# Eight modulation vectors of a two-block attention stage, taken from VectorE's multiply-adds to TensorE's float32 products

## The chip, the cores and the metric

The kernel runs on one core of a Trainium2 chip. The metric is device time in microseconds, the median of three runs. The engines named below are TensorE (PE, with its weight loads as PEld), VectorE (DVE), ScalarE (ACT), GpSimd (POOL) and SyncE (SP), which only issues transfers here.

## What is computed

512 tokens of 1,024 channels go through four layers of the same shape. The mixer of the first is MLA and sliding-window attention, of the second differential and forgetting attention, of the last two a convolution and a gated recurrence, each of these with an MLP behind it. Each layer is modulated by vectors that come from a conditioning vector c:

```
ada   = silu(c) @ w_ada + b_ada          # 1024 -> 3 * 1024 for an attention layer
h     = rmsnorm(x, g_pre) * (1 + scale) + shift
x'    = x + gate * rmsnorm(mixer(h) @ w_out, g_post)
```

A vector is 1,024 columns of such a product: 4 MB of float32 weights, read once. This study is about eight of those vectors: gate 0 with its g_post, and scale and shift of the second layer, and one vector for a later layer, all made while the first attention mixer runs; and the gate of the second layer and scale, shift and gate of the third, made while the second attention mixer runs.

## The kernel before

Everything large is a product on TensorE. Each float32 operand is split into a high and a low part and the product is taken as three products of the parts (L207, `mm3`); the splits are made by ACT (L199, L221) and by DVE or POOL (L200, L224). The program is written in layer order, and a list scheduler with a model of its own for times sets the order on each engine. Every engine then takes its instructions strictly in that order: an instruction that waits holds up all that stand behind it on its engine.

The four functions that matter:

- `even` and `odd` are the two attention mixers. Scores go through TensorE (psum tag `sc`), a softmax that alternates between DVE (L596 maximum and mask, L599 reciprocal), ACT (L598 exponential) and POOL (L603 scaling), a transpose of the probabilities on TensorE (L626, tag `tp`) and a product with V (L636, L645, tag `pv`). In between stand products of the weights for gates and projections (tag `mm`), which need no softmax. Query and key heads are transposed by `heads_T` (L613) into the psum tag `tq`, of which there is one bank.
- `ada` queues a vector in eight steps, two halves of 512 columns by four steps of 256 rows. A step loads 256 x 512 weights (512 KB) with one transfer on SP's queue (L497) into one of two buffers called `araw`, and DVE adds two 128 x 512 multiples of it to `acc` (L502 for the first one of a half, L504 for the others). Behind the fourth step of a half four products of a column of ones (L511, each into its own 32 columns of the array) sum `acc` over the partitions, DVE adds the bias (L513) and multiplies by g where there is one (L517), and four transfers of 512 bytes write the row to DRAM (L520).
- `tick` takes the next step from the queue; `group` calls it after each group of products of a weight, the mixers call it after a head, `flush` takes what is left. So the steps lie between the softmaxes in the order of DVE.
- `first` runs a mixer with its four vectors queued before it or by it, and afterwards spreads the rows over the partitions (L547) for the out projection.

In both mixers 32 steps are taken, so the study is about 64 steps, 128 multiply-adds on DVE and 16 groups of four products of ones. The vectors of the later layers use the same function and are not touched.

Of the kernel before, what the change touches and what calls it, by code (L numbers as in the profile page):

```python
# [16 lines left out]
P = 128  # L17
# [9 lines left out]
# layout of the constant array  # L27
# [39 lines left out]
G0 = 2  # L67
LEVELS = (1, 2, 4, 8, 16, 32, 64, 128, 256)
# [8 lines left out]
def constants():  # L77
# [16 lines left out]
    # of a row's block of 32: the columns of each level; of a row's block of 128: the block of 32 on the diagonal  # L94
# [13 lines left out]
def cap4(v, o):  # L108
    """512 elements of a DRAM vector as four rows of 128, each on 32 partitions"""
    return bass.AP(tensor=v.tensor, offset=v.offset + o, ap=[[P, 4], [0, 32], [1, P]])  # L110


class K:
    def __init__(self, tc, h, es):
# [12 lines left out]
        self.ada_pool = ()  # L127
        self.ada_tag, self.ada_raw = "mm", ("araw", 2)
# [18 lines left out]
    def scope(self, **bufs):  # L147
        """a pool of working tiles; bufs by tag"""
# [26 lines left out]
    def oT_tiles(self, t0):  # L175
        """a mixer's output as a split pair: the first token block in t0, the others in the places of the activations
        that the mixer read"""
        act = self.act

        class O:  # L180
            def __init__(self, a):
                self.a = a

            def __getitem__(self, ix):
                _, k, t = ix
                if t.start >= P:
                    return act[self.a][:, k, t]
                return t0[self.a][:, k, t]
        return O(0), O(1)
# [19 lines left out]
    def wgran(self, w, k0, nk, c0, cw, own=False):  # L209
        """weights rows [k0*128, (k0+nk)*128), cols [c0, c0+cw) -> split pair [128, 2, nk, cw]"""  # L210
# [16 lines left out]
    def wload(self, w, c0, cw, kc, own=0):  # L227
        """the weights of kc chunks of channels, the last granules in own tiles of the scope"""
# [9 lines left out]
    def rank(self, off):  # L238
        """instructions that the scheduler takes off places later than their place in the program"""
# [5 lines left out]
    def mark(self):  # L245
        """what comes from the queue of the modulation stays behind the work of DVE so far"""
# [6 lines left out]
    def advance(self, g, have, want):  # L253
        """steps of g until their cost reaches want; the cost so far"""
# [7 lines left out]
    def weave(self, main, n, fill, cost):  # L262
        """n steps of main, with fill of that cost (or of cost(i) after i steps) spread over them, and kept behind
        them on TensorE"""
# [22 lines left out]
    def gemm_xs(self, act, w, c0, cw, kc, evac, tag="mm", subs=None):  # L287
        """out[tok, c0:c0+cw] by token block; evac(tb, psums)"""
# [17 lines left out]
    def gemm_xk(self, act, gs, cw, kc, evac):  # L306
        """as gemm_x, with the channels outermost"""
# [9 lines left out]
    def gemm_tb(self, act, w, evac, after=None, late=None):  # L317
        """out[tok, 0:1024], a token block's two halves one after the other; evac(tb, half, psum). with late,
        the last channels come late: the first half of two token blocks does the others first, the second block after
        that instruction"""  # L320
# [29 lines left out]
    def gemm_ws(self, act, w, c0, cw, kc, evac, tag="mm"):  # L350
        """out[c0:c0+cw, tok] by chunks of 128 channels; evac(chunk, psum)"""
# [14 lines left out]
    def gemm_wh(self, act, jobs):  # L366
        """as gemm_w for jobs (w, c0, evac) of 256 channels, the first half of the tokens before the second"""
# [14 lines left out]
    def rstd(self, ss, n, cols=1):  # L382
        """(ss/n + eps)^-1/2"""
# [8 lines left out]
    def cond(self, cs):  # L392
        """silu of each vector of cs, as columns [128, 8]"""
# [10 lines left out]
    def start(self, x_in, c, c2, w, b, g, wg, cw):  # L404
        """norm and modulation of the first layer: the normalised x channel-major while the modulation's weights
        come in; returns silu(c) and the step that makes chunk k of the split pair"""
# [77 lines left out]
    def ada(self, ccol, w, b, c0, kind, g=None):  # L484
        """one vector of the modulation as a row in DRAM, queued in eight steps"""
# [3 lines left out]

        def step(half, gk):  # L490
            o0 = c0 + half * 512
# [3 lines left out]
            tag, n = self.ada_raw  # L495
            raw = self.wp.tile([P, 2, 512], F32, tag=tag, name=self.nm(tag), bufs=n)
            nc.sync.dma_start(out=raw, in_=w[gk * 256:(gk + 1) * 256, o0:o0 + 512].rearrange("(k p) c -> p k c", p=P))  # L497
# [9 lines left out]
            arow = self.rp.tile([P, P], F32, tag="arow", name=self.nm("arow"), bufs=2)  # L507
            nc.sync.dma_start(out=arow, in_=cap4(b, o0))
# [5 lines left out]
            if g is not None:  # L514
                gr = self.rp.tile([P, P], F32, tag="gr", name=self.nm("gr"), bufs=2)
                nc.sync.dma_start(out=gr, in_=cap4(g, half * 512))
                nc.vector.scalar_tensor_tensor(out=arow, in0=arow, scalar=1.0 if kind == "scale" else 0.0, in1=gr,  # L517
                                               op0=ALU.add, op1=ALU.mult)
            for j in range(4):
                nc.sync.dma_start(out=row[half * 512 + j * P:half * 512 + (j + 1) * P].unsqueeze(0), in_=arow[32 * j:32 * j + 1])  # L520

        def later(h_, q_):
            if STRICT:
                self.mark()
            with self.tc.issue_after(self.gate):
                step(h_, q_)
# [9 lines left out]
    def group(self):  # L536
        """after each group of products of a weight"""
# [3 lines left out]

    def flush(self):
        self.tick(len(self.pend))

# [1243 lines left out]
```

## Time and profile before

| | before |
|---|---|
| time of three runs | 2110.22, 2113.64 (median), 2122.06 us |
| span of the profiled execution | 2106.4 us (its own time is not listed beside it) |
| mean granted TensorE clock | 0.959 |
| busy share of the span | PE 92%, DVE 67%, ACT 42%, POOL 38% |
| transfers | 270.67 MB, 128 GB/s in the mean |
| attention mixers with the 64 steps | about 46 to 700 us |

The median stands 7.2 us above the span of the profiled execution; a span is therefore compared with a span, and 7.2 us is added to get to a time of a run. Busy times are of an execution that was profiled; the granted clock is the share of full speed that TensorE was given, 1.00 for 2.4 GHz and 0.50 for 1.2 GHz.

### The profile page before, as it was taken

How to read it: one execution, taken by the hardware profiler on the slowest of the kernel's cores; microseconds unless marked ns; L12 is line 12 of the kernel's file. 1: busy time of each engine (PE TensorE's matmuls, PEld its weight loads, DVE VectorE, ACT ScalarE, POOL GpSimd, SP SyncE). 2: the span in 40 equal slices, each digit the busy share in tenths (PEclk: the TensorE clock that was granted, in tenths of full speed). 3: DMA queues.
4: the chain of work that ended last, by engine and by line, in shares of the span. 5: the costliest groups of instructions: out<-in, count | busy, mean ns of one | idle time of the engine just before them, and what ended most of it. 6: DMA issues, size and time to landing. Idle time of an engine off the chain costs nothing.

```text
span 2106.4 us, 32096 instructions
## 1 busy us (share of the span) xinstructions
PE 1943.9 (92%) x12471; PEld 1580.0 (75%) x12471; DVE 1402.8 (67%) x1987; ACT 884.5 (42%) x1499; POOL 805.1 (38%) x701
## 2 busy tenths in 40 slices
PE   7799999897999988679899999999999998999998
PEld 5688667664776776448788989876777778898896
DVE  5356775545555769976987648667787858485673
ACT  4245553134544434333525436243454534352452
POOL 1223334222233448615232422455585544223232
PEclk9899979998999999889999999999999999999999
DMA  8384555366343751432554235453322322242331
GB/s 317 121 230 142 173 165 157 88 156 144 87 129 94 250 165 56 110 105 91 170 187 132 83 99 178 132 151 106 101 78 87 116 86 80 90 131 71 121 101 60
DMA packets 225024, 270.67 MB, mean 128 GB/s; under 512 B 26602, under 2 KB 145609, under 8 KB 224872
## 3 DMA queue, kind: packets, MB, share of 16 engines
q1 hardware_dynamic: 188982, 232.83, 36.3%
q10 hardware_dynamic: 35890, 35.79, 5.5%
q8 instruction: 98, 1.61, 0.3%
q14 instruction: 54, 0.44, 0.1%
HBM read 252.46 MB, written 16.12 MB: 128 GB/s over the span
## 4 chain that ended last, share of the span: by engine, by line
PE 49%; DVE 14%; issue 6%; DMA 6%; POOL 4%; ACT 2%; ACTq 0%; POOLq 0%; DVEq 0%; SPq 0%
PE mm L207 28%; PE sc L207 5%; PE mm L1186 4%; PE sc L1186 3%; PE tp L1186 3%; DVE acc L504 3%; DMA araw<-in_ada_w_dram 2%; DVE hl L224 2%; DVE ol L1312 2%; DVE hl L200 1%; DMA raw<-in_od_w_in_dram 1%; DVE X L1547 1%; PE pv L207 1%; DMA raw<-in_ada_w_dram 1%; PE tp L626 1%
## 5 line engine op out<-in xcount | busy, mean ns | idle before, releaser
L207 PE MATMUL mm<-hTh,hl 128*128 128x512 f32 (+1 forms) x1296 | 410.9, 393 | 19.0 <-ACT t L1339 7.0
L207 PE MATMUL mm<-hl,hid 128*128 128x512 f32 x1344 | 317.0, 395 | 5.3 <-DVE hid L200 3.8
L221 ACT CAST hl<-raw 128x1024 fp32r<-128x1024 f32 (+2 forms) x219 | 224.1, 1033 | 223.8 <-PE mm L207 133.8
L207 PEld LDWEIGHTS mm<-hl,hid 128*128 128x128 f32 x1344 | 251.9, 188 | 65.2 <-DVE hid L200 4.9
L207 PEld LDWEIGHTS mm<-hTh,hl 128*128 128x128 f32 x1296 | 242.8, 194 | 74.6 <-ACT t L1339 7.9
L224 DVE TENSOR_TENSOR hl<-raw,hl 128x1024 fp32r<-128x1024 f32 (+2 forms) x186 | 251.3, 1361 | 67.3 <-ACT hl L221 66.8
L207 PE MATMUL mm<-hTl,hl 128*128 128x512 f32 (+2 forms) x648 | 253.2, 391 | 0.9 <-DVE hTl L200 0.8
L207 PE MATMUL mm<-hl,hTh 128*128 128x512 f32 (+3 forms) x752 | 220.5, 371 | 26.9 <-DVE t L584 11.9
L1103 POOL TENSOR_TENSOR xr<-xr,t 128x512 f32<-128x512 f32 x56 | 80.4, 1435 | 303.4 <-DVE t L1100 303.4
L504 DVE SCALAR_TENSOR_TENSOR acc<-araw,ccol,acc 128x512 f32<-128x512 f32 x182 | 158.5, 871 | 45.0 <-DMA araw<-in_ada_w_dram 31.4
L207 PEld LDWEIGHTS mm<-hl,hTh 128*128 128x128 f32 x752 | 140.0, 197 | 52.2 <-ACT t L751 9.6
L603 POOL TENSOR_TENSOR s<-s,sm 128x256 f32<-128x256 f32 (+3 forms) x112 | 82.7, 739 | 184.0 <-DVE sm L599 165.4
L207 PEld LDWEIGHTS mm<-hTl,hl 128*128 128x128 f32 (+1 forms) x648 | 125.6, 194 | 26.4 <-DVE hTl L200 1.5
L199 ACT CAST hl<-raw 128x1024 fp32r<-128x1024 f32 x84 | 86.8, 1048 | 136.1 <-PE mm L207 111.3
L200 DVE TENSOR_TENSOR hl<-raw,hl 128x1024 fp32r<-128x1024 f32 x84 | 131.3, 1578 | 13.5 <-ACT hl L199 12.9
L207 PE MATMUL mm<-hl,hTl 128*128 128x512 f32 (+3 forms) x376 | 138.8, 369 | 0.3 <-DVE hTl L457 0.3
L224 POOL TENSOR_TENSOR hl<-raw,hl 128x1024 fp32r<-128x1024 f32 x33 | 84.3, 2554 | 131.5 <-ACT hl L221 131.4
L1166 POOL TENSOR_TENSOR raw<-raw,raw 128x1024 f32<-128x1024 f32 x28 | 76.2, 2722 | 147.1 <-DVE rows L1166 85.2
L1100 DVE TENSOR_TENSOR t<-mm,rows 128x512 f32<-128x512 f32 x56 | 38.5, 687 | 104.3 <-PE mm L207 104.0
L598 ACT ACTIVATE s<-s,sm 128x256 f32<-128x256 f32 (+5 forms) x128 | 69.6, 544 | 90.7 <-DVE sm L596 86.7
L1312 DVE SCALAR_TENSOR_TENSOR ol<-u,dw,ol 128x512 f32<-128x512 f32 x90 | 103.2, 1147 | 2.9
L207 PE MATMUL sc<-b,b 64*128 64x256 f32 (+7 forms) x384 | 92.2, 356 | 12.5 <-DVE sm L596 11.7
(358 smaller groups left out, 3956.4 us busy)
## 6 DMA issues: line engine op xcount, KB each, us to landing
raw<-in_mlp_w_dram SPq DMA_DIRECT2D x128, 512.0 KB
araw<-in_ada_w_dram SPq DMA_DIRECT2D x72, 512.0 KB
raw<-in_hgrn_w_in_dram SPq DMA_DIRECT2D x40, 512.0 KB
araw<-in_w_ada_dram SPq DMA_DIRECT2D x32, 512.0 KB
raw<-in_od_w_in_dram SPq DMA_DIRECT2D x32, 512.0 KB
raw<-in_ada_w_dram SPq DMA_DIRECT2D x24, 512.0 KB
rows<-row SPq DMA_DIRECT2D x16, 512.0 KB
raw<-in_conv_w_in_dram SPq DMA_DIRECT2D x16, 512.0 KB
```

The costliest lines, as they stand in the source:

```text
L199: nc.scalar.copy(out=hi, in_=src)
L200: nc.vector.tensor_tensor(out=lo, in0=src, in1=hi.bitcast(F32), op=ALU.subtract)
L207: self.nc.tensor.matmul(out, lhsT=lt[a], rhs=rt[b], start=start and n == 0, stop=stop and n == 2)
L221: self.nc.scalar.copy(out=hi, in_=raw[:, :n])
L224: eng.tensor_tensor(out=lo, in0=raw[:, :n], in1=hi.bitcast(F32), op=ALU.subtract)
L504: eng.scalar_tensor_tensor(out=acc, in0=raw[:, k], scalar=c, in1=acc, op0=ALU.mult, op1=ALU.add)
L598: nc.scalar.activation(out=s[:, :m], in_=s[:, :m], func=AF.Exp, scale=-1.0, bias=mn, accum_out=sm)
L603: nc.gpsimd.tensor_tensor(out=p, in0=p, in1=r.to_broadcast([P, n]), op=ALU.mult)
L1103: eng.tensor_tensor(out=xs, in0=xs, in1=t, op=ALU.add)
L1166: eng.tensor_tensor(out=out, in0=x, in1=y, op=f)
L1186: nc.tensor.matmul(ps[:, m * 256:m * 256 + 256], lhsT=ws[n][:, a, k, m * P:m * P + P], rhs=parts[n][b][:, k], start=m + k + t == 0, stop=m ...
L1312: nc.vector.scalar_tensor_tensor(out=yc, in0=u[:, j:j + T], scalar=dw[:, cc, j:j + 1], in1=yc, op0=ALU.mult, op1=ALU.add)
```

## The change

In the two attention mixers, and only there, a step is made on TensorE. After the 512 KB load eight float32 products per step go through the array, for two blocks of 128 rows and four groups of 32 columns: the column of silu(c) stands as the weights, repeated over 32 columns, and a raw 128 x 128 block of `araw` streams through. The eight products of a step gather in the single `tq` bank, and DVE adds the 128 x 128 result to `arow`, which starts as the bias. The products of a step are written one tick later than its load (`ADA_LAG`), and the last ones in `flush`. The bias is now loaded at the first step of a half. The ones, `acc` and its 128 x 512 multiply-adds are gone from these 64 steps.

```diff
+        def step_pe(half, gk):
+            if gk == 0:
+                st[half] = bias(half)
+            raw = load(half, gk)
+            def products():
+                ps = self.psum(self.ada_ps)
+                for k in range(2):
+                    for j in range(4):
+                        nc.tensor.matmul(ps[32 * j:32 * j + 32, :P], lhsT=cap(ccol, gk * 2 + k, [(0, 32)]),
+                                         rhs=raw[:, k, j * P:(j + 1) * P], start=k == 0, stop=k == 1, tile_position=(0, 32 * j))
+                nc.vector.tensor_tensor(out=st[half], in0=ps[:, :P], in1=st[half], op=ALU.add)
+                if gk == 3:
+                    finish(half, st[half])
+            self.ada_late.append(products)
+            self.ada_do(ADA_LAG)
...
-                step(h_, q_)
+                (step_pe if self.ada_pe else step)(h_, q_)
...
+    def ada_do(self, keep):
+        while len(self.ada_late) > keep:
+            self.ada_late.pop(0)()
...
     def flush(self):
         self.tick(len(self.pend))
+        with self.tc.issue_after(self.gate):
+            self.ada_do(0)
...
+                    k.ada_pe = True
...
+                    k.ada_pe = False
```

`load`, `bias` and `finish` hold the lines that `step` had for its load, its bias and the end of a half. The lines of the changed kernel are numbered otherwise: the products of a step stand in L523 and the add in L525, the three-term products in L209, the softmax in L634 (maximum) and L637 (reciprocal), its combination in the differential attention in L1034 and L1035, the transpose of probabilities in L664.

On DVE, in the differential attention of the second mixer, this is the order of before; `s` and `sm` belong to the softmax, `b` is a split pair from the `tq` bank, `acc` and `araw` are the step's:

```order
L596 ISA sm_4299 128x1
L599 RECIPROCAL sm_4301<-sm_4300 128x1
L596 ISA s_4306,sm_4307<-sc_4294,cst 128x128
L596 ISA sm_4307 128x1
L203 SCALAR_TENSOR_TENSOR b_1019_4383<-tq_4378,b_1019_4383 128x512
L599 RECIPROCAL sm_4309<-sm_4308 128x1
L504 SCALAR_TENSOR_TENSOR acc_4550<-araw_4801,ccol_93,acc_4550 128x512
L996 TENSOR_TENSOR sm_4313<-sm_4309,nlam 128x1
L596 ISA s_4350,sm_4351<-sc_4342,cst 128x256
```

At the same place on DVE the order of the change is this:

```order
L634 ISA sm_4531 128x1
L637 RECIPROCAL sm_4533<-sm_4532 128x1
L634 ISA s_4538,sm_4539<-sc_4526,cst 128x128
L634 ISA sm_4539 128x1
L205 SCALAR_TENSOR_TENSOR b_1038_4615<-tq_4610,b_1038_4615 128x512
L637 RECIPROCAL sm_4541<-sm_4540 128x1
L1034 TENSOR_TENSOR sm_4545<-sm_4541,nlam 128x1
L634 ISA s_4582,sm_4583<-sc_4574,cst 128x256
```

The multiply-add that stood ahead of the next softmax is gone; the next add of a step (L525) stands some fifteen rows further on.

On TensorE the order of the change in the first mixer, where the MLA heads end and the sliding window's begin, has products of four steps close together (`araw_2019`, `araw_2123`, `araw_2200` and `araw_2214` are four loads that follow one another through the two buffers):

```order
L209 MATMUL sc_2309<-b_426_1994,b_424_1986 128x256 x3
L523 MATMUL tq_2125<-araw_2019,ccol_93 32x128 x8
L209 MATMUL sc_2247<-b_450_2092,b_448_2084 128x128 x2
L523 MATMUL tq_2202<-araw_2123,ccol_93 32x128 x8
L209 MATMUL sc_2321<-b_450_2092,b_448_2084 128x256 x3
L209 MATMUL sc_2356<-b_426_1994,b_424_1986 128x384 x3
L664 MATMUL tp_2263<-cst,s_2251 128x128
L523 MATMUL tq_2216<-araw_2200,ccol_93 32x128 x8
L209 MATMUL sc_2368<-b_450_2092,b_448_2084 128x384 x3
L664 MATMUL tp_2333<-cst,s_2313 128x128 x2
L683 MATMUL pv_2234<-pt_2265,V_939 64x128
L209 MATMUL sc_2427<-b_426_1994,b_424_1986 128x512 x3
```

Before, there was no instruction on TensorE here that reads `araw`; now a group of eight stands between the scores.

In the sliding-window heads of the first mixer TensorE had one group of ones in such a stretch before (`SV` is the window's V, `acc` the sum of four steps):

```order
L207 MATMUL sc_2919<-b_545_2424,b_634_2702 128x256 x3
L626 MATMUL tp_2842<-cst,s_2828 128x128 x2
L511 MATMUL mm_3252<-acc_3067,ones 32x128 x4
L207 MATMUL sc_2932<-b_545_2424,b_651_2759 128x256 x3
L207 MATMUL sc_2962<-b_545_2424,b_634_2702 128x256 x3
```

It has a step's products after every second or third group of scores in the change:

```order
L664 MATMUL tp_3037<-cst,s_3015 128x128
L523 MATMUL tq_3193<-araw_2997,ccol_93 32x128 x8
L209 MATMUL sc_3102<-b_553_2523,b_643_2813 128x256 x3
L683 MATMUL pv_2768<-pt_2956,SV_753 64x128
L683 MATMUL pv_2768<-pt_2951,SV_753 64x128
L683 MATMUL pv_2768<-pt_2956,SV_753 64x128
L664 MATMUL tp_3041<-cst,s_3028 128x128
L523 MATMUL tq_3207<-araw_3191,ccol_93 32x128 x8
L209 MATMUL sc_3115<-b_553_2523,b_660_2870 128x256 x3
```

So the first mixer's products no longer start with its first gates: the first one stands behind some 490 of TensorE's rows, all 32 steps of this mixer lie in rows 492 to 906, and eleven of them, with the first step of the second mixer as a twelfth, in rows 820 to 915. The 32 of the second mixer lie in rows 915 to 2040, most with 7 to 20 us of other TensorE work between a step and the next but one.

## Rows read from the trace of the kernel before

**Rows 1.** The page's busy times: share of the span, number of instructions.

```profile
PE 1943.9 (92%) x12471; PEld 1580.0 (75%) x12471; DVE 1402.8 (67%) x1987; ACT 884.5 (42%) x1499; POOL 805.1 (38%) x701
```

**Rows 2.** The page's chain that ended last, by engine and by line.

```profile
PE 49%; DVE 14%; issue 6%; DMA 6%; POOL 4%; ACT 2%; ACTq 0%; POOLq 0%; DVEq 0%; SPq 0%
PE mm L207 28%; PE sc L207 5%; PE mm L1186 4%; PE sc L1186 3%; PE tp L1186 3%; DVE acc L504 3%; DMA araw<-in_ada_w_dram 2%; DVE hl L224 2%; DVE ol L1312 2%; DVE hl L200 1%; DMA raw<-in_od_w_in_dram 1%; DVE X L1547 1%; PE pv L207 1%; DMA raw<-in_ada_w_dram 1%; PE tp L626 1%
```

**Rows 3.** Windows of 53 us: busy time of each engine, granted clock, DMA share.

```profile
core 0: us, PE busy (x) PEld busy (x) DVE busy (x) ACT busy (x) POOL busy (x), PEclk, DMA share, GB/s
...
212.00:265.00 53.00, 51.38 (x337) 36.99 (x336) 40.59 (x111) 28.94 (x80) 19.61 (x38) 1.00 0.58 171
265.00:318.00 53.00, 51.16 (x249) 34.27 (x248) 38.04 (x98) 26.90 (x76) 17.41 (x38) 0.74 0.54 169
...
477.00:530.00 53.00, 38.63 (x160) 27.88 (x161) 28.32 (x80) 21.59 (x48) 11.29 (x10) 0.81 0.57 134
```

**Rows 4.** Groups by line on DVE, 30 to 720 us.

```profile
L504 DVE SCALAR_TENSOR_TENSOR acc<-araw,ccol,acc 128x512 f32<-128x512 f32 x127 | 104.4, 822 | 38.1 <-DMA araw<-in_ada_w_dram 25.0 <-DMA araw<-in_w_ada_dram 12.3
...
L513 DVE TENSOR_TENSOR arow<-mm,arow 128x128 f32<-128x128 f32 x16 | 4.6, 288 | 6.3 <-PE mm L511 6.3
```

**Rows 5.** TensorE's timeline: four-column-group products of the kernel's start (two records each).

```profile
start us, us, engine line op out<-in xcount [idle before <-releaser]
...
25.94 0.65 PE L433 MATMUL pv<-wide,rep 128*32 128x128 f32 x16
26.52 0.66 PE L473 MATMUL tp<-cst,t 128*128 128x128 f32 x4
...
30.68 1.08 PE L433 MATMUL tq<-wide,rep 128*32 128x128 f32 x16
31.70 0.69 PE L207 MATMUL mm<-hl,hTl 128*128 128x384 f32 x1
...
35.94 1.08 PE L433 MATMUL tq<-wide,rep 128*32 128x128 f32 x32
36.95 0.44 PE L207 MATMUL mm<-hl,hTh 128*128 128x384 f32 x1
```

**Rows 6.** TensorE's timeline around one group of ones.

```profile
258.39 0.39 PE L207 MATMUL mm<-hTl,hl 128*128 128x512 f32 x1
258.62 0.39 PE L207 MATMUL mm<-hTh,hl 128*128 128x512 f32 x1
258.94 0.42 PE L511 MATMUL mm<-acc,ones 128*32 128x128 f32 x8
259.30 0.43 PE L645 MATMUL pv<-pt,SV 128*64 128x128 f32 x2
```

**Rows 7.** Timeline of SP, DVE and TensorE at 473 to 483 us.

```profile
473.62 0.44 SPq L497 DMA_DIRECT2D araw<-in_ada_w_dram  x1
...
481.56 0.75 DVE L504 SCALAR_TENSOR_TENSOR acc<-araw,ccol,acc 128x512 f32<-128x512 f32 x1 [5.86 <-DMA araw<-in_ada_w_dram]
...
482.78 1.32 PE L207 MATMUL sc<-b,b 64*128 64x384 f32 x3 [6.43 <-DVE sm L596]
```

**Rows 8.** The same engines at 499 to 509 us.

```profile
499.13 0.40 SPq L497 DMA_DIRECT2D araw<-in_ada_w_dram  x1
...
507.47 0.75 DVE L504 SCALAR_TENSOR_TENSOR acc<-araw,ccol,acc 128x512 f32<-128x512 f32 x1 [4.24 <-DMA araw<-in_ada_w_dram]
...
508.55 1.00 PE L207 MATMUL sc<-b,b 64*128 64x256 f32 x3 [3.94 <-DVE sm L596]
```

**Rows 9.** TensorE's timeline: two other waits in the second mixer.

```profile
460.06 0.50 PE L207 MATMUL mm<-hTh,hl 128*128 128x512 f32 x1 [4.24 <-DVE o L668]
...
525.48 0.90 PE L626 MATMUL tp<-cst,s 128*128 128x128 f32 x3 [3.90 <-DMA raw<-in_od_w_in_dram]
```

**Rows 10.** SP's and DVE's timeline in the first mixer's sliding window: two loads.

```profile
278.56 0.40 SPq L497 DMA_DIRECT2D araw<-in_ada_w_dram  x1
...
282.56 0.75 DVE L504 SCALAR_TENSOR_TENSOR acc<-araw,ccol,acc 128x512 f32<-128x512 f32 x1 [0.39 <-DMA araw<-in_ada_w_dram]
...
281.73 0.37 SPq L497 DMA_DIRECT2D araw<-in_ada_w_dram  x1
...
286.35 0.75 DVE L504 SCALAR_TENSOR_TENSOR acc<-araw,ccol,acc 128x512 f32<-128x512 f32 x1 [1.22 <-DMA araw<-in_ada_w_dram]
```

**Rows 11.** Windows of 10 us, columns as in rows 3.

```profile
150.00:160.00 10.00, 7.60 (x38) 6.12 (x37) 8.96 (x19) 4.21 (x12) 4.05 (x3) 0.84 0.70 208
...
280.00:290.00 10.00, 10.00 (x42) 6.31 (x40) 7.34 (x24) 5.15 (x17) 4.19 (x11) 0.50 0.68 216
```

More of the change, by code (lines that the diff above doesn't have):

```diff
@@ L67 @@
 G0 = 2
+ADA_LAG = 1
 LEVELS = (1, 2, 4, 8, 16, 32, 64, 128, 256)
@@ L127, in __init__ @@
         self.ada_pool = ()
+        self.ada_pe, self.ada_late, self.ada_ps = False, [], "tq"
         self.ada_tag, self.ada_raw = "mm", ("araw", 2)
@@ L488, in ada, with load, bias, finish @@
         st = {}
+        def load(half, gk):
+            o0 = c0 + half * 512
+            tag, n = self.ada_raw
+            raw = self.wp.tile([P, 2, 512], F32, tag=tag, name=self.nm(tag), bufs=n)
+            nc.sync.dma_start(out=raw, in_=w[gk * 256:(gk + 1) * 256, o0:o0 + 512].rearrange("(k p) c -> p k c", p=P))
+            return raw
+        def bias(half):
+            arow = self.rp.tile([P, P], F32, tag="arow", name=self.nm("arow"), bufs=2)
+            nc.sync.dma_start(out=arow, in_=cap4(b, c0 + half * 512))
+            return arow
+        def finish(half, arow):
+            if g is not None:
+                gr = self.rp.tile([P, P], F32, tag="gr", name=self.nm("gr"), bufs=2)
+                nc.sync.dma_start(out=gr, in_=cap4(g, half * 512))
+                nc.vector.scalar_tensor_tensor(out=arow, in0=arow, scalar=1.0 if kind == "scale" else 0.0, in1=gr,
+                                               op0=ALU.add, op1=ALU.mult)
+            for j in range(4):
+                nc.sync.dma_start(out=row[half * 512 + j * P:half * 512 + (j + 1) * P].unsqueeze(0), in_=arow[32 * j:32 * j + 1])
+        def step_pe(half, gk):
[5 more added lines that the diff above has]
+                for k in range(2):
+                    for j in range(4):
+                        nc.tensor.matmul(ps[32 * j:32 * j + 32, :P], lhsT=cap(ccol, gk * 2 + k, [(0, 32)]),
[5 more added lines that the diff above has]
+            self.ada_do(ADA_LAG)
         def step(half, gk):
-            o0 = c0 + half * 512
             if gk == 0:
@@ L494, in step @@
             acc = st[half]
-            tag, n = self.ada_raw
-            raw = self.wp.tile([P, 2, 512], F32, tag=tag, name=self.nm(tag), bufs=n)
-            nc.sync.dma_start(out=raw, in_=w[gk * 256:(gk + 1) * 256, o0:o0 + 512].rearrange("(k p) c -> p k c", p=P))
+            raw = load(half, gk)
             for k in range(2):
@@ L506, in step @@
                 return
-            arow = self.rp.tile([P, P], F32, tag="arow", name=self.nm("arow"), bufs=2)
-            nc.sync.dma_start(out=arow, in_=cap4(b, o0))
+            arow = bias(half)
             ps = self.psum(self.ada_tag)
@@ L513, in step @@
             nc.vector.tensor_tensor(out=arow, in0=ps[:, :P], in1=arow, op=ALU.add)
[L514 to L520, printed above, removed]
+            finish(half, arow)
         def later(h_, q_):
```

## The prediction

> **What bounds the kernel now.** I read the busy times first. TensorE is busy for 92% of the span, VectorE for 67% [rows 1], so a microsecond taken from VectorE is worth something only where TensorE waits for it, and a microsecond given to TensorE costs nearly all of itself. The chain that ended last says the same: half of it is TensorE, and the multiply-adds and their loads, the two entries that the change touches, are 3% and 2%, some 100 us together [rows 2]. That is not a gain in waiting: where a chain runs over a multiply-add, TensorE was often busy beside it.
>
> So I went to windows over the two mixers, and there the shares differ. In the first mixer TensorE has hardly a gap: 51.38 of 53 us between 212 and 265 us, though VectorE is at its busiest with 40.59 [rows 3]. From 265 to 318 us it is as full, 51.16, but at a granted clock of 0.74 [rows 3]; inside, from 280 to 290 us, it is busy for all 10 us at 0.50 [rows 11], that is 1.2 GHz, after a wait of the scores on VectorE. In the second mixer there are real gaps: 38.63 of 53 us from 477 to 530, at a clock of 0.81 [rows 3]. VectorE is not full there, 28.32 us; it stands still. The waits tell why: at 481.56 a multiply-add has waited 5.86 us for its load, issued at 473.62, and behind it stands the softmax; TensorE's scores start at 482.78 after 6.43 us of idleness, for that softmax [rows 7]. At 507.47 the same: 4.24 us for a load issued at 499.13, and TensorE 3.94 us later than it could [rows 8]. The order shows the multiply-add ahead of the softmax there before, and gone in the change.
>
> **What it costs on TensorE.** 64 steps of eight products. The trace has the same form (128 rows, 32 columns, 128x128 streamed, two records per product) at the kernel's start: one group of 16 records starts at 25.94 and the next instruction at 26.52, so a step is 0.58 us; a run of two such groups goes from 35.94 to 36.95, 0.505 each; at a lower clock a group takes 30.68 to 31.70, 1.02 [rows 5]. I take 0.58, since nearly every step stands alone: 64 x 0.58 = 37.1 us (32.3 by the packed price). The Trainium skill says in "TensorEngine Tiling (Array Packing)", Tiling Modes, that changing the tiling mode drains TensorE. The trace agrees in size: the lone group is 0.075 us dearer than the packed one; by that rule the sum is the 37.1 taken here, without it 32.3.
>
> Taken away: 16 groups of ones, 258.94 to 259.30, 0.36 each [rows 6], 5.8 us. Left are **+31.3 us**, if all of it lies on TensorE's path. In the second mixer some of it falls into gaps that stay: of the 14.4 us idle from 477 to 530 [rows 3] about 10 are the two waits above; I put **-4** for products that fill the rest and gaps like it.
>
> **What it costs in waits.** *The tq bank.* One bank, shared with the transposes of heads; the next user waits for VectorE's add, 0.29 us (the add behind the ones has the same shape [rows 4]) plus what VectorE has in hand. Most uses are far apart; some six come close (the order shows transposes into tq just ahead of a step): **+2**, 0 to 8.
>
> *Loads that TensorE now waits for itself.* A step's load can start only when the products of the step but one before have read its buffer. Two loads in the sliding window took 282.56 - 278.56 = 4.0 and 286.35 - 281.73 = 4.6 us from issue to use [rows 10]. Between the products on `araw_2019` and those on `araw_2200` the order has 128 x 2 + 256 x 3 + 384 x 3 columns, a step and a transpose. A product of 512 columns takes 0.23 us (258.39 to 258.62 [rows 6]), so that is 1.0 + 0.58 + about 0.2 = 1.8 us, and TensorE would stand still for 2.2 to 2.8. Done so for each step, with the durations of such rows, the steps up to row 761 of the first mixer wait 4.7 us at 4.0 per load and 7.0 at 4.6; part of it lies in gaps that are there anyway: **+4**, 0 to 7. Rows 820 to 915 have some 23 us of work for twelve steps; at full clock they would wait 9 to 13 us.
>
> *That stretch and its clock.* Today its work runs partly at 0.50; from 265 to 318 the lost clock is worth (1 - 0.74) x 51.16 = 13.3 us [rows 3]. If the clock stays up, 13.3 comes back and 9 to 13 goes into waits: -4 to 0. If it stays low, loads are in time, but twelve products cost 1.02 instead of 0.58: +5. I take **0**.
>
> **What it gives back.** VectorE is rid of 127 multiply-adds of 0.82 us, 104.4 us [rows 4], and gets 48 more small adds of 0.29. Where TensorE was the one to wait:
> - 150 to 160 us, eight multiply-adds in a burst: 2.4 us idle, and (1 - 0.84) x 7.60 = 1.2 of clock [rows 11]: **-3.6**.
> - 212 to 265 us: 1.6 us idle [rows 3]: **-1.6**.
> - Second mixer: the two direct waits, 6.43 + 3.94 = 10.4 [rows 7, 8]; of the lost clock from 477 to 530, (1 - 0.81) x 38.63 = 7.3 [rows 3], 80%: 5.8; of the waits of 4.24 and 3.90 [rows 9], which hang on VectorE through other steps or on a weight's transfer, half: 4.1. Together **-20.3**, between -12 and -26.
>
> **Sum.** 31.3 - 4 + 2 + 4 + 0 - 3.6 - 1.6 - 20.3 = +7.8 us. Span 2106.4 + 7.8 = 2114.2; the median stands 7.2 above the span, so 2121.4, say 2121 us: 0.4% slower, within the 0.5% (10.6 us) below which a measurement of this kernel can't tell a change from none.
>
> **Rivals.**
> - *All stalls of VectorE come back, nothing new waits.* Products at the packed price (26.5 net), no tq wait, -4 for gaps, -4 in the sliding window, -3.6 - 1.6, and all of 10.4 + 7.3 + 8.1 = 25.8 in the second mixer: -12.5, thus 2101 us; with the full 13.3 of clock in the sliding window 2092. For it: VectorE's line is on the chain [rows 2]. Against: the price on TensorE is sure, and a clock that rises there makes loads late.
> - *The first mixer starves on its loads* (the other side). Loads of 4.6 us and more, one after the other through two buffers: +7 and +13 in the two dense stretches with the clock low around them so that nothing of the 13.3 returns, tq at +8, and the second mixer gives 16: 31.3 - 4 + 8 + 20 - 3.6 - 16 = +36, 2149 us; halfway between it and the forecast 2135. It decides from a landing of about 4.6 us on. For it: the order's dense places. Against: half clock stretches the work between loads.
> - *The wait only moves.* The loads of 473.62 and 499.13 took 7.9 and 8.3 us [rows 7, 8]; if those of the change are issued no earlier, TensorE waits at L523 instead of VectorE, and the second mixer gives 5 instead of 20.3: +23, 2137 us. Against: 7 to 20 us of work stand between a step and the next but one there, and a softmax no longer stands behind the load.
>
> **How the numbers follow.** The forecast, a balance within 0.5%: 0.36. All stalls back, 2088 to 2103: 0.30. Starved first mixer: 0.20, and the wait that moves: 0.14, both from 2124 to 2149. So faster 0.30, same 0.36, slower 0.34. The range leaves out a tenth at each end: 2088 to 2144; the forecast's own is 2104 to 2124.
>
> **What would show it.** Products at L523 of 0.55 to 0.6 us each at full clock, about 37 us of busy time. In the second mixer no score waits over 3 us for a softmax; 477 to 530 at a clock above 0.9 if the balance holds. In the first mixer, L523 waiting for `araw` at rows 699 to 730 and 820 to 915: some 4 and some 9 us, or the stretch at half clock without waits. It goes wrong most easily by the clock in the sliding window, worth 13 us either way, and by landings of 8 us where I count with 4.

## The result, and the profile after

The changed kernel takes 2170.63 us (median of 4 runs, 2164.54 to 2184.58) against 2116.65 us before (4 runs, 2110.22 to 2122.06): a ratio of 1.0279, interval 1.0247 to 1.0312. It is 2.8% slower, 54 us between the medians and 59 by the ratio, where I had forecast a balance within 0.5% and no more than 2144 us. The profiled executions have spans of 2169.1 and 2106.4 us: 62.7 us to account for. Some of these are chance: where a run lists both, its time is about 2 us above its span, so the profiled execution of before took some 2108 us, less than any of the four timed ones (most of the 7.2 us by which the median stood above the span is this), while that of the change, 2170.91 us, is close to its median.

The busy times of the page of the changed kernel, as [rows 1] of before:

```profile
PE 2004.7 (92%) x13367; PEld 1610.9 (74%) x13367; DVE 1331.6 (61%) x1907; ACT 886.7 (41%) x1499; POOL 799.1 (37%) x701
```

TensorE has 60.8 us more of busy time, VectorE 71.2 less. Read like this the change costs what TensorE got, and nothing waits. That reading is too simple, as the experiments show. To see where the time went I cut both traces at a place that both have, the first product of each out projection (operand `oT`). TensorE's timeline of the changed kernel at those two places:

```profile
350.73 0.73 PE L209 MATMUL mm<-hl,oT 128*128 128x512 f32 x2 [0.74 <-ACT oT L201]
...
746.03 0.73 PE L209 MATMUL mm<-hl,oT 128*128 128x512 f32 x2
```

Before they stand at 308.35 and 694.88 us. The windows over the two mixers, from 106 us (up to there the two traces run alike) to the first out projection, and from behind its last transposes (349.92 us before, 392.68 in the change) to the second, of the kernel before:

```profile
core 0: us, PE busy (x) PEld busy (x) DVE busy (x) ACT busy (x) POOL busy (x), PEclk, DMA share, GB/s
106.00:308.35 202.35, 196.48 (x1160) 149.66 (x1158) 134.04 (x347) 101.26 (x269) 70.69 (x112) 0.92 0.61 176
349.92:694.88 344.96, 310.88 (x1528) 226.45 (x1525) 184.53 (x412) 141.17 (x288) 99.83 (x90) 0.95 0.46 121
```

And of the changed kernel:

```profile
106.00:350.73 244.73, 228.15 (x1606) 168.54 (x1604) 98.17 (x307) 102.03 (x269) 64.17 (x112) 0.87 0.50 142
392.68:746.03 353.35, 333.11 (x1954) 234.76 (x1952) 150.12 (x374) 141.07 (x287) 98.28 (x90) 0.97 0.51 119
```

The first mixer is 42.4 us longer, the second 8.4, the two out projections 2.2, and the layers behind them, whose program is nearly the same, 9.8. In the first mixer TensorE's idle time grew from 5.9 to 16.6 us and its clock fell from 0.92 to 0.87; what the clock costs, (1 - 0.87) x 228.15 against (1 - 0.92) x 196.48, is 29.7 us instead of 15.7. So about 11 us of the 42 are idle time, 14 are clock, and the rest is about the products less the ones. VectorE is busy for 98 of 245 us. In the second mixer it is the other way: idle from 34.1 to 20.2 us and a clock of 0.97. The windows that answer to [rows 3] show the same at a glance:

```profile
212.00:265.00 53.00, 47.52 (x332) 32.64 (x335) 18.82 (x63) 20.30 (x52) 11.90 (x20) 0.77 0.48 136
265.00:318.00 53.00, 48.79 (x321) 31.95 (x314) 18.98 (x71) 18.72 (x57) 11.40 (x31) 0.74 0.34 95
530.00:583.00 53.00, 49.10 (x298) 35.23 (x297) 18.52 (x67) 24.01 (x51) 8.37 (x9) 0.97 0.57 93
```

From 212 to 265 us, where [rows 3] had 51.38 busy at a clock of 1.00, there are 47.52 at 0.77, and VectorE has less than half of its 40.59. No other engine is busy for half of the stretch; something waits in a ring.

The products themselves, taken one by one, are as priced. All of their line, in both mixers (idle before them, by what ended it; then who waited for them):

```profile
L523 PE MATMUL tq<-araw,ccol x1024: 269/273/424, 179.0 to 739.7; 128*32 128x128 f32 x171
...
  DMA araw<-in_w_ada_dram: 1.7, 3
  DMA araw<-in_ada_w_dram: 1.7, 3
...
  DVE arow L525: 67.3, 39
```

TensorE's own waits for late loads are 3.4 us in all. VectorE waited 67.3 us for products, 39 times, with softmaxes behind the add. One such place in the first mixer, in the timeline of TensorE, VectorE, ScalarE and GpSimd:

```profile
226.64 0.29 DVE L525 TENSOR_TENSOR arow<-tq,arow 128x128 f32<-128x128 f32 x1 [0.80 <-PE tq L523]
...
228.03 0.60 PE L651 MATMUL tq<-cst,t 128*96 128x128 f32 x4
...
231.26 0.64 PE L651 MATMUL tq<-cst,t 128*96 128x128 f32 x4
...
237.04 0.64 PE L523 MATMUL tq<-araw,ccol 128*32 128x128 f32 x16
237.75 0.29 DVE L525 TENSOR_TENSOR arow<-tq,arow 128x128 f32<-128x128 f32 x1 [4.51 <-PE tq L523]
...
237.98 0.55 PE L209 MATMUL sc<-b,b 96*128 96x128 f32 x3
...
238.88 0.60 PE L651 MATMUL tq<-cst,t 128*96 128x128 f32 x4
...
242.08 0.40 POOL L641 TENSOR_TENSOR s<-s,sm 128x128 f32<-128x128 f32 x1 [15.06 <-DVE sm L637]
...
242.54 0.33 PE L664 MATMUL tp<-cst,s 128*128 128x128 f32 x1 [3.06 <-POOL s L641]
...
242.70 0.86 PE L651 MATMUL tq<-cst,t 128*96 128x128 f32 x4
...
244.24 1.22 PE L209 MATMUL sc<-b,b 96*128 96x128 f32 x4
```

Everything in tq comes in a row here: a step and its add, the two transposes of one head of a pair, a step and its add, the first scores of that head, the two transposes of the other head, and only then its scores. GpSimd had no softmax to scale for 15 us, TensorE stands for 3.06 us, and its granted clock, 1.00 from 230 to 240 us, is 0.5 in the next steps (one takes 1.01 us at 245.39). My first reading was that the add does it: it waits 4.51 us in VectorE's order, ahead of softmaxes. The experiments say otherwise.

### The profile page after: what moved, and what is told of

It is laid out like the page before. It is cut to its first block, busy times and chain, and to the rows that moved or that the text cites. A ratio compares the mean times of both kernels' runs of the same rounds, so it can differ in the third digit from the quotient of the medians.

```text
span 2169.1 us, 33841 instructions
## 1 busy us (share of the span) xinstructions
PE 2004.7 (92%) x13367; PEld 1610.9 (74%) x13367; DVE 1331.6 (61%) x1907; ACT 886.7 (41%) x1499; POOL 799.1 (37%) x701
## 4 chain that ended last, share of the span: by engine, by line
PE 52%; DVE 12%; DMA 5%; issue 4%; POOL 4%; ACT 2%; ACTq 0%; POOLq 0%; SPq 0%; DVEq 0%
PE mm L209 28%; PE sc L209 6%; PE mm L1224 4%; PE sc L1224 3%; PE tp L1224 3%; DVE acc L543 3%; DVE ol L1350 2%; DVE hl L226 1%; PE pv L209 1%; DMA raw<-in_ada_w_dram 1%; DVE hl L202 1%; PE tq L523 1%; DVE X L1585 1%; DMA araw<-in_ada_w_dram 1%; PE tp L664 1%
## 5 line engine op out<-in xcount | busy, mean ns | idle before, releaser
L209 PE MATMUL mm<-hTh,hl 128*128 128x512 f32 (+1 forms) x1296 | 413.5, 395 | 13.6 <-ACT t L1377 5.8
L209 PE MATMUL mm<-hl,hid 128*128 128x512 f32 x1344 | 316.9, 395 | 2.1 <-DVE hid L202 1.7
L209 PEld LDWEIGHTS mm<-hl,hid 128*128 128x128 f32 x1344 | 251.9, 188 | 61.9 <-DVE hid L202 2.8
L209 PEld LDWEIGHTS mm<-hTh,hl 128*128 128x128 f32 x1296 | 243.6, 194 | 72.3 <-issue 6.9
L209 PE MATMUL mm<-hTl,hl 128*128 128x512 f32 (+2 forms) x648 | 255.2, 394 | 1.8 <-DVE hTl L202 1.7
L209 PE MATMUL mm<-hl,hTh 128*128 128x512 f32 (+3 forms) x752 | 225.3, 376 | 22.4 <-DVE t L622 8.2
L209 PEld LDWEIGHTS mm<-hl,hTh 128*128 128x128 f32 x752 | 143.0, 202 | 47.6 <-ACT t L789 8.4
L641 POOL TENSOR_TENSOR s<-s,sm 128x256 f32<-128x256 f32 (+3 forms) x112 | 75.9, 678 | 242.4 <-DVE sm L637 239.5
L209 PEld LDWEIGHTS mm<-hTl,hl 128*128 128x128 f32 (+1 forms) x648 | 126.1, 195 | 27.6 <-DVE hTl L202 2.4
L209 PE MATMUL mm<-hl,hTl 128*128 128x512 f32 (+3 forms) x376 | 140.1, 373 | 0.0
L209 PE MATMUL sc<-b,b 64*128 64x256 f32 (+7 forms) x384 | 95.0, 368 | 4.7 <-DVE sm L634 2.2
L1588 POOL TENSOR_TENSOR X<-X,T 128x512 f32<-128x512 f32 x56 | 74.8, 1340 | 50.7 <-ACT op L1548 32.8
```

Source lines behind the costliest of these rows:

```text
L209: self.nc.tensor.matmul(out, lhsT=lt[a], rhs=rt[b], start=start and n == 0, stop=stop and n == 2)
L641: nc.gpsimd.tensor_tensor(out=p, in0=p, in1=r.to_broadcast([P, n]), op=ALU.mult)
L1588: nc.gpsimd.tensor_tensor(out=xk, in0=xk, in1=cap(Tt, 1, [(row - 1, 2), (2, nb), (0, hh)]), op=ALU.mult)
```

## The experiments

Of each run: the median, the ratio to the kernel before with its interval, and the length of the two mixers cut as above (before 202.4 and 345.0 us, the change 244.7 and 353.4). The lengths are of the one execution that was profiled, which is up to 12 us from the run's median. Every edit also lets the scheduler order the rest anew, so no run changes one thing alone.

**Each mixer alone.** `k.ada_pe = True` is replaced.

```diff
-                    k.ada_pe = True
+                    k.ada_pe = i == 0
```

> Products on TensorE in the first mixer only; the second mixer's 32 steps are VectorE multiply-adds again. Theory A (the loss is made in the first mixer, where its 32 steps are pressed between 179 and 352 us): spread of the first rows (L585) near 351 us as in the change, and a time some 45 us over before, about 2155 to 2165. Theory B (the products cost about the same TensorE time wherever they stand, half of the loss in each mixer): some 27 us over before, about 2143.

```diff
-                    k.ada_pe = True
+                    k.ada_pe = i == 1
```

> Products on TensorE in the second mixer only. Theory A: the first mixer ends near 305 us as before; what is left is the second mixer's 15.6 us of products less the waits that VectorE no longer makes, 5 to 15 us over before, about 2120 to 2130. Theory B: some 27 us over before, about 2143.

The first alone: 2150.32 us, 1.0180 (1.0138 to 1.0222), mixers 237.8 and 344.8. The second alone: 2134.05 us, 1.0099 (1.0066 to 1.0131), mixers 207.3 and 349.5. The two losses add up to that of the change, nearly two thirds from the steps of the first mixer. Neither theory had the size of either: both times lie between the two forecasts. With the steps of the second mixer alone that mixer is only 4.5 us longer, but the first, into which five of the steps are drawn, is 4.9 longer, and the layers behind the mixers 6.

**Earlier steps.** The first mixer's queue is also served between its first weight products.

```diff
-                    k.tick_every = TO if i else 1000
+                    k.tick_every = TO if i else 2
```

> All 64 steps on TensorE, but the first mixer takes a step after every second group of weight products from its start, so that 14 of its 32 steps stand in TensorE's first 360 rows instead of behind row 490. Theory A (place): 14 steps fall where TensorE had gaps or dense weight products, fewer stand between the softmaxes: the first rows are spread at 325 to 338 us, total 2145 to 2160. Theory B (time of the products): no change against the changed kernel, 2165 to 2175.

2163.82 us, 1.0238 (1.0199 to 1.0277), mixers 239.6 and 349.8: 7 us less than the change, between the two forecasts; taking the steps earlier helps little. Place is not the main cause.

**No products.** The add reads a part of the loaded weights.

```diff
-                        nc.tensor.matmul(ps[32 * j:32 * j + 32, :P], lhsT=cap(ccol, gk * 2 + k, [(0, 32)]),
-                                         rhs=raw[:, k, j * P:(j + 1) * P], start=k == 0, stop=k == 1, tile_position=(0, 32 * j))
-                nc.vector.tensor_tensor(out=st[half], in0=ps[:, :P], in1=st[half], op=ALU.add)
+                nc.vector.tensor_tensor(out=st[half], in0=raw[:, 0, :P], in1=st[half], op=ALU.add)
```

> The 512 products are left out: the small add reads a 128 x 128 part of the loaded weights instead of the sum of products, so the modulation vectors are wrong; loads, adds, rows stay. If TensorE's time for products and what follows from it is the whole loss, the time falls to 2085 to 2105 (below before by the relief of VectorE, 10 to 30 us). If the loss comes from the order of the rest (weight products bunched elsewhere, loads later), it stays over 2130.

2111.85 us, 0.9978 (0.9958 to 0.9997). Its two windows:

```profile
106.00:320.83 214.83, 198.89 (x1103) 150.83 (x1101) 110.23 (x337) 101.75 (x270) 67.27 (x113) 0.90 0.75 231
362.48:694.15 331.67, 309.87 (x1479) 225.34 (x1477) 151.19 (x358) 141.42 (x287) 99.54 (x90) 0.96 0.35 88
```

In this order VectorE's relief and the missing ones bring 13.3 us in the second mixer and nothing in the first, which is 12.5 us longer; 9 of these are over before its first softmax, with the loads denser (231 GB/s against 176), which may be the reason but was not tested. The time is neither of the two forecasts (2085 to 2105, or over 2130). The whole gain is 0.22% (0.03 to 0.42), some 5 us; with the rest ordered like this, the change could pay only if all 512 products cost less than that.

**No add, the add elsewhere, one add.** First the small add is left out, so nobody reads the products and the rows hold the bias alone.

```diff
-                nc.vector.tensor_tensor(out=st[half], in0=ps[:, :P], in1=st[half], op=ALU.add)
```

> All 512 products of the change stay on TensorE, in nearly the same places, but VectorE's 64 small adds are left out, so nobody reads the products and the modulation rows hold only the bias (times g). Theory C (the add stands in VectorE's order in front of softmaxes and waits for a product that stands behind weight products on TensorE, so softmax and TensorE are tied together): the first mixer loses most of its 42 us, its out projection starts near 320 to 330 us, total 2130 to 2148. Theory D (the products' own time and the lower clock that they bring): adds change nothing, 2160 to 2172.

2175.56 us, 1.0307 (1.0267 to 1.0346), mixers 246.2 and 352.6: no gain at all. So the wait of 67.3 us of VectorE does not make the loss, and theory C falls. The add by way of ScalarE and GpSimd:

```diff
-                nc.vector.tensor_tensor(out=st[half], in0=ps[:, :P], in1=st[half], op=ALU.add)
+                e_ = self.rp.tile([P, P], F32, tag="gr", name=self.nm("gr"), bufs=2); nc.scalar.copy(out=e_, in_=ps[:, :P])
+                nc.gpsimd.tensor_tensor(out=st[half], in0=e_, in1=st[half], op=ALU.add)
```

> The change with the add taken from VectorE: ScalarE copies the sum of a step out of tq, GpSimd adds it to the row. Theory C in its narrow form (VectorE is the engine that must not wait): 2140 to 2155. If the wait only moves to ScalarE, whose exponentials are in the same softmax chain: 2160 to 2180. Theory D: 2160 to 2172.

2175.68 us, 1.0296 (1.0263 to 1.0329), mixers 237.0 and 357.3: no gain in the whole. Then the bank is kept for the steps, with one add per half; the heads' transposes (and the head norms of these mixers) go to tp:

```diff
-                ps = self.psum(self.ada_ps)
+                if gk == 0:
+                    st[half, 1] = self.psum(self.ada_ps)
+                ps = st[half, 1]
...
-                                         rhs=raw[:, k, j * P:(j + 1) * P], start=k == 0, stop=k == 1, tile_position=(0, 32 * j))
+                                         rhs=raw[:, k, j * P:(j + 1) * P], start=gk + k == 0, stop=gk + k == 4, tile_position=(0, 32 * j))
-                nc.vector.tensor_tensor(out=st[half], in0=ps[:, :P], in1=st[half], op=ALU.add)
                 if gk == 3:
+                    nc.vector.tensor_tensor(out=st[half], in0=ps[:, :P], in1=st[half], op=ALU.add)
...
-        ps = self.psum("tq")
+        ps = self.psum("tp")
...
+                    k.alts["hn"] = ["tp"]
...
+                    k.alts["hn"] = ["tq"]
```

> The change with the tq bank kept for the steps alone (the transposes of heads and the head norms of these two mixers use tp): the 32 products of a half gather in it over its four steps, and VectorE adds once per half, 16 adds instead of 64; correct as it stands. Theory C: most of the first mixer's loss goes, 2130 to 2150, unless the transposes now wait for each other in tp. Theory D: 2160 to 2172.

2153.72 us, 1.0204 (1.0169 to 1.0239), mixers 227.6 and 358.1. The first mixer got 17 us back, by one of two edits: fewer adds or the bank.

**Products beside the old way, and products twice.** In the kernel before, each step's products are made as well and read by nobody.

```diff
+            if self.ada_pe:
+                ps = self.psum("tq")
+                for k in range(2):
+                    for j in range(4):
+                        nc.tensor.matmul(ps[32 * j:32 * j + 32, :P], lhsT=cap(ccol, gk * 2 + k, [(0, 32)]),
+                                         rhs=raw[:, k, j * P:(j + 1) * P], start=k == 0, stop=k == 1, tile_position=(0, 32 * j))
...
+                    k.ada_pe = True
...
+                    k.ada_pe = False
```

> The kernel before, whole, with the change's 512 products beside it: each step's products also go into the tq bank, and nobody reads them. VectorE keeps its multiply-adds and waits for nothing new. Theory C: 64 x 0.57 = 36 us at most, less what falls into gaps: 2135 to 2150, the first mixer some 18 us longer than before. Theory D: as dear as in the change or dearer, 55 us and more: 2165 to 2180.

2197.95 us, 1.0411 (1.0373 to 1.0449), mixers 236.1 and 383.0: dearer than the change, 83 us for 36 us of products, with no add that waits. It seemed to speak for theory D, the products' own time and clock. Why the second mixer is 38 us longer here no run tells. Then the change with each step's products made twice:

```diff
-                for k in range(2):
+                for k in (0, 1, 0, 1):
```

> The change with every step's eight products made twice, the second time anew, so the result stands: the marginal price of a step. If a step costs its 0.57 us and no more: 36 us over the change, 2205. If products also cost clock or waits in proportion (in the change a step costs 0.85 us over before): 54 us, 2225. If much falls into idle places: under 2195.

2184.38 us, 1.0344 (1.0323 to 1.0365): only 14 us over the change. Its window of the first mixer, and one of a pause between two softmaxes in it:

```profile
106.00:349.45 243.45, 227.65 (x2055) 171.65 (x2053) 98.64 (x305) 102.61 (x269) 63.77 (x112) 0.94 0.49 140
...
258.05:273.22 15.17, 10.75 (x154) 7.70 (x154) 4.92 (x16) 5.32 (x11) 3.21 (x9) 1.00 0.59 173
```

With nearly twice the products (60 groups of eight instead of 32) the first mixer takes 243.45 us instead of 244.73, TensorE is busy for the same 228 us, and the granted clock is 0.94 instead of 0.87. So the time of products does not simply add up here, though TensorE is busy for 93% of the stretch: the 15 us that these groups take more (38 against 23 by the starts) are what the lost clock gives back, (1 - 0.94) x 227.65 = 13.7 us instead of 29.7. That fits a length that something else sets, with TensorE's work at half clock stretched to fill it; and the long pauses between softmaxes, of which more below, stay (11.4, 17.8 and 15.2 us), the third of them with a clock of 1.00 and TensorE idle for 4.4 us. Theory D, by which products cost in proportion, falls too. That the clock rose by chance as much as the work grew is not excluded by one run.

**The bank.** Heads' transposes and head norms in tp, steps alone in tq with their 64 adds:

```diff
-        ps = self.psum("tq")
+        ps = self.psum("tp")
...
+                    k.alts["hn"] = ["tp"]
...
+                    k.alts["hn"] = ["tq"]
```

> The change with the tq bank for the steps alone (transposes of heads and the head norms of these mixers go to tp), 64 adds on VectorE as in the change. Theory E (what costs beyond the products is the tq bank: a step's products and the transposes of heads wait for each other and for the evictions): as the run with one add per half, the first mixer some 26 us over before, total 2150 to 2160. If the number of adds was what helped there: 2165 to 2175.

2139.35 us, 1.0131 (1.0111 to 1.0151), mixers 219.4 and 347.4: 31 us better than the change, better than with one add and than either forecast. The same move in the kernel before, as a control:

> A control: the kernel before with the transposes of heads and these mixers' head norms in tp instead of tq, nothing else. If the bank is free of cost or gain by itself: 2105 to 2125. If it gains 10 us or more by itself, what the runs with an own bank gained says nothing of the steps.

2136.63 us, 1.0120 (1.0085 to 1.0155), mixers 218.8 and 350.8. The move alone costs the kernel before 1.2%, which neither forecast had, and with it made in both, the change costs 2.7 us in all, within the noise of the two. The windows of the first mixer, with the steps in a bank of their own and of the control:

```profile
106.00:325.40 219.40, 210.87 (x1588) 156.16 (x1587) 95.75 (x304) 102.87 (x268) 63.02 (x112) 0.95 0.55 155
...
106.00:324.81 218.81, 205.54 (x1160) 153.54 (x1158) 133.46 (x348) 101.82 (x269) 71.43 (x112) 0.88 0.59 169
```

So the run with an own bank shows that products can be hidden nearly whole beside heads that are slow already, but not against the kernel before. The loads left out, with the products reading a resident identity:

```diff
-            raw = load(half, gk)
...
-                                         rhs=raw[:, k, j * P:(j + 1) * P], start=k == 0, stop=k == 1, tile_position=(0, 32 * j))
+                                         rhs=self.ident, start=k == 0, stop=k == 1, tile_position=(0, 32 * j))
```

> The change without the 64 loads of weights: the products read a resident identity instead of the loaded block, so the modulation rows are wrong; products, adds and rows stay. Theory G (TensorE, in order, waits for late loads and all stands behind): the first mixer keeps only its 18 us of products and about 3, total 2135 to 2150. Theory E: the bank still ties, 2160 to 2172.

2146.27 us, 1.0156 (1.0132 to 1.0180), mixers 232.3 and 345.5. The loads are worth 12 us of the first mixer and 8 of the second, more than TensorE's own 3.4 us of waiting for them, but 30 us of loss stay in the first. The total is in the range of theory G; its account, 18 + 3 us over before in the first mixer, is not met.

Then the heads stay in tq, and the sums of the steps go to each other pair of banks, mm as below, tp and sc likewise:

```diff
-        self.ada_pe, self.ada_late, self.ada_ps = False, [], "tq"
+        self.ada_pe, self.ada_late, self.ada_ps = False, [], "mm"
```

> The change with the sums of the steps in the two mm banks (of the weight products) and the heads in tq as before. Theory E (the single tq bank, shared with the heads' transposes, is what costs): the first mixer at most 20 us over before, total 2110 to 2140. If any shared bank costs as much: 2160 and more.

> The same with the sums in the two tp banks (of the transposed probabilities). Theory E: 2110 to 2140; but tp is on the softmax chain, and a step that waits for its load holds a tp bank, so nearer to the upper end than the run in mm. If any shared bank costs as much: 2160 and more.

> The same with the sums in the two sc banks (of the scores). Theory E: 2110 to 2145, at the upper end, since scores feed the softmax. If any shared bank costs as much: 2160 and more.

In mm: 2178.06 us, 1.0321 (1.0278 to 1.0365), mixers 216.1 and 377.1. In tp: 2147.48 us, 1.0169 (1.0133 to 1.0204), mixers 215.7 and 349.1. In sc: 2161.36 us, 1.0233 (1.0199 to 1.0268), mixers 218.6 and 360.5. The windows of the run in tp:

```profile
106.00:321.74 215.74, 208.49 (x1518) 157.56 (x1517) 93.39 (x299) 100.08 (x267) 62.30 (x112) 0.91 0.51 146
367.71:716.78 349.07, 328.79 (x1956) 235.77 (x1954) 148.34 (x370) 142.96 (x288) 98.21 (x90) 0.96 0.50 117
```

In all three the first mixer is 13 to 16 us longer than before instead of 42, which is about what the 27 to 32 steps in it cost at 0.57 (15 to 18 us); theory E had at most 20. The whole kernel doesn't follow: no run is in the range of theory E, and mm and sc are where any shared bank was to cost as much. There the second mixer pays (32 and 16 us over before), and in all three the layers behind the mixers are 19 to 23 us longer than before, against 9.8 in the change. In mm the second mixer has 12.3 us in which TensorE waits for loads and 15.3 for VectorE to read a weight product, I suppose since a step that waits for its load holds a bank of the weight products.

Why the one bank costs so much stands in the order. For the transposes of heads in the first mixer, in their order, I counted in the traces how many tiles of scores TensorE has begun ahead of each (a head pair's scores begin at 8, 16, 24 and 32; the third row is of three runs, with early steps, with no loads and with products twice):

```
before               0 0 1 1 3 5 7 9 11 12 15 17 19 21 23 25 27 28 30 32 34
the change           0 0 1 1 3 5 7 9 16 16 17 17 24 24 25 25 32 32 33 42 44
early, no loads, x2  0 0 1 1 3 5 7 9 16 16 17 17 24 24 25 25 32 32 33 42-43 44-46
heads in tp, before  0 0 1 1 8 8 9 9 15 16 17 17 23 24 25 25 32 32 32 45 47
no products          0 0 1 1 3 5 7 9 10 13 15 17 19 21 23 25 27 29 30 32 34
steps in tp          0 0 1 1 3 5 7 9 11 13 16 17 19 21 23 25 27 29 30 32 33
steps in mm          0 0 1 1 3 5 7 9 11 13 15 17 19 21 23 25 27 31 32 35 37
steps in sc          0 0 1 1 3 5 6 8 9 10 14 16 16 17 18 24 25 27 29 32 35
```

With tq to themselves the transposes run ahead: at the eleventh tile those of the pair that begins at the sixteenth. In the change the tiles of the one bank are used in turn, steps and heads, and all four transposes of a pair come when its scores are due: at 16, 24, 32. Then transposes, evictions, scores and softmax of a pair follow one another with nothing of the next pair ready. VectorE's softmaxes show it. Counted from 0 and from end to end of their maxima, the 14th and the 16th lie 4.9 us apart before and 12.7 in the change, the 22nd and the 24th 5.8 and 15.9, the 30th and the 32nd 4.0 and 17.5; in between they run alike (18.0 and 17.3 us from the 24th to the 30th). With the steps in tp, where the transposes run ahead, the three are 3.5, 4.2 and 4.8. The 30th and the 32nd, before and in the change:

```profile
237.03 0.67 DVE L596 CUSTOM_DVE_ANT_0 s<-sc,cst 128x512 f32<-128x512 f32 x1
...
241.37 0.33 DVE L596 CUSTOM_DVE_ANT_0 s<-sc,cst,nsink 128x128 f32<-128x128 f32 x1
...
255.64 0.69 DVE L634 CUSTOM_DVE_ANT_0 s<-sc,cst 128x512 f32<-128x512 f32 x1 [1.08 <-POOL s L641]
...
273.48 0.35 DVE L634 CUSTOM_DVE_ANT_0 s<-sc,cst,nsink 128x128 f32<-128x128 f32 x1 [1.11 <-PE sc L209]
```

The three pauses together are 31.4 us longer than before, and the 32nd softmax starts 32 us later; the other 10 us of the first mixer come behind it. TensorE need not be idle in such a pause: in the second one of the change it does other work all the time, at a clock of 1.00.

```profile
223.07:238.98 15.91, 15.91 (x129) 11.84 (x128) 4.13 (x14) 4.84 (x10) 2.41 (x3) 1.00 0.42 120
```

That this work is then missing later, where TensorE is idle or at half clock, I infer. The control, the kernel before with heads in tp, has late transposes too and loses 16.5 us in the first mixer without any product.

No version beats the kernel before, and the runs point to none: the relief is worth 13 us, seen in the second mixer alone, and a mixer's products take 15 to 25.

## Why the prediction was wrong

- **The tq bank**, "+2, 0 to 8", is the step that failed. I priced each handover of the bank by one add (0.29 us) and asked only how often two uses come close. What it does is to fix an order: transposes that ran a head pair ahead are late. Measured by the other banks (215.7 to 218.6 us for the first mixer against 244.7) it costs 26 to 29 us there. The order of TensorE would have told it, had I counted the scores ahead of each transpose in both kernels; the rows of it that I showed hold the steps and no transpose into tq.
- **What bounds the first mixer.** I read 51.38 and 51.16 busy us of 53 [rows 3] as a full TensorE. As long as the heads run ahead this holds about: with the steps in other banks the first mixer grows by about what its products take. I carried it over to the change, where it fails: with 93% busy, 28 groups more took no time.
- **The price of products**, 0.58 a step, was right where a step stands alone: 0.57 from start to next start, 1.01 at half clock. Over all it was 48 us instead of 37.1 (22.9 in the first mixer, 0.6 between, 24.5 in the second, by the starts), eight of the first mixer's steps at half clock, and the second mixer's 31 steps cut into 51 groups, 0.34 for a piece of two records. The Trainium skill ("TensorEngine Tiling (Array Packing)", Key Properties) says that a change of the tiling mode drains TensorE; the trace fits it: a piece of two of 16 records, with a change before and behind it, costs more than half of the whole group. I had that rule and did not see that the order cuts groups.
- **Loads that TensorE waits for**: 3.4 us of direct waits, against +4 and up to 13 counted. Without loads the two mixers are 12.4 and 7.9 us shorter, so they delay more than they show, I suppose by the bank that a waiting step holds; the size was near, by another way.
- **The sliding window's clock**, taken as 0 between -4 and +5, came out low: 0.50 from 280 to 300 us. The late heads are not needed for that: the kernel before is at 0.50 there too, and the run with the steps in tp, whose heads are early, from 290 to 320 us; with the steps in mm the first mixer's clock is 0.99. What decides it stays open.
- **VectorE's relief in the second mixer** was right in kind: its scores waited 11.4 us for VectorE before, 0.3 now.

```profile
L207 PE MATMUL sc<-b,b 64*128 64x128 f32 (+3 forms) x192 | 45.5, 358 | 11.4 <-DVE sm L596 10.6 <-DVE b L200 0.9
...
L209 PE MATMUL sc<-b,b 64*128 64x128 f32 (+3 forms) x192 | 44.0, 356 | 0.3 <-DVE sm L634 0.2
```

  Its size was less: 13.3 us with the ones instead of 20.3 + 2.9. In the first mixer I counted -5.2, and the run without products shows none. The 127 multiply-adds of [rows 4] were misread too, without a term in the sum: they take in later vectors, and the 64 steps have 112 of that line and 16 of L502.
- **The later layers**, 9.8 us of the loss, were in no term. Their program is the same but for the places of later vectors' steps, and in the other runs they differ from before by -1 to +23 us. In the 150 us from the second out projection's start VectorE had 24 multiply-adds of later vectors before and 28 after, and the convolution keeps it busy (46.64 of 50 us from 788 us on, before). But the run with the steps in tp has 24 there too and loses 19 us behind its mixers, so this does not explain it; a part may be the execution that happened to be profiled. The cause stays open.
- The rival of a starved first mixer had the sign and most of the place (2149 us), but loads for a cause, which are 12 of its 42 us; the one in which the wait only moves did not happen: the second mixer's scores no longer wait.

What stays open: how the 26 to 29 us divide between late transposes (16 us by the control) and the bank held by steps that wait, since the two were not separated in tq; and why the whole kernel wins back 23 us with the steps in tp, 9 in sc and none in mm.

## What to carry to other kernels

A buffer with one place is an order: before putting new users into it, count what its old users run ahead of, and whether they still can. Busy time of TensorE at half clock need not be a full TensorE: double the work that is suspected, and if the stretch gets no longer and the clock rises, look for the bound elsewhere. And price the relief by itself (the work taken from the other engine, with nothing in its place) before arguing about the cost, with an eye on what else moved; here the loads did.

## What the runs showed of the hardware

A group of 16 records of these products, each into 32 columns of the array, costs 0.57 us from start to next start at a granted clock of 1.00, 1.01 at 0.50, and a piece of two records between other products 0.34. In one run more work on TensorE in the same time went with a higher granted clock, 0.94 against 0.87, and 28 groups more took no time. The small add on VectorE that reads the bank takes 0.29 us and waited up to 6.7 us for its product; with all 64 left out the kernel was no faster (2175.56 us).
